# Two modulation steps ahead of the first projection, keys split two tiles at a time, the last blocks' product with v and the last norm by halves

## The chip, the core and the metric

The kernel runs on one core of a Trainium2 chip. A core has four engines that compute: TensorE (PE: matmuls and transposes, with weight loads listed apart as PEld), VectorE (DVE), ScalarE (ACT) and GpSimd (POOL). SyncE (SP) issues most transfers. Each engine takes its instructions in the order of its own list and waits on semaphores that other engines or transfers raise. The time is device microseconds for one launch of the program; before is the median of 3 runs.

## What is computed

One layer of a hybrid backbone block over 512 latent and 256 context tokens of width 1024, all in f32. Cut to what matters here:

```python
mod = silu(c) @ w_mod + b_mod            # shift, scale, gate; twice
h = x * (1 + sc1) + sh1                  # and the context with its own
z = h @ w_in                             # q, k, v, o, gates of the mLSTM; q, k, v of the attention
hm = mlstm_bidir(silu(conv(z_qk)), z_v, gates)
qa, ka = rope(rms_norm(z_qa)), rope(rms_norm(z_ka))
att = softmax(qa @ ka.T * scale) @ va    # 8 query heads, 2 heads of keys
mix = concat([sigmoid(o) * norm(hm), att]) @ w_out
x = layer_norm(ALPHA * x + g1 * mix)
y = peer(x * (1 + sc2) + sh2)            # per token: gelu(u[idx] . x) * g, times v[idx]
x = layer_norm(ALPHA * x + g2 * y)
```

PEER looks up, for each token, 8 x 16 of 16384 experts; each expert has a row u (dotted with the token) and a row v (added, weighted).

## The kernel before

Tokens lie in tiles of 128 (`NCH` = 6 with the context, `NT` = 4 latent). The kernel is one long program written in stages; within a stage a scheduler has already interleaved the engines' instructions, so the lists below are what each engine runs.

**Projections.** `ORDER` (L71) is a string of steps, each run in turn. K, A, B, Q, R, C, D, O and P are column groups of `w_in` (K: keys and values of the attention and the gates; A to D: the mLSTM's q and k, with the convolution on DVE; Q and R: the attention's q; O and P: the output gate, with a sigmoid on ACT). `load_cols` loads 1 MB into a slot `wi` (L206), ACT casts it to a high part `whi` (L208), POOL subtracts to get a low part `wlo` (L209), each in two halves, and PE makes three products (high x high, high x low, low x high; L219). The step m is `mod_rows`: a 1 MB load `wm` of the modulation's weights (L419) into the same three `wi` slots, and two products with a running sum on DVE, `mod_col` (L151). There are 16 such steps; those not in `ORDER` follow at its end (`more_rows(16)`). g and s are the gates' and the states' parts of the mLSTM; k and q are norm and rope of the attention's keys and queries, on DVE, with Newton steps for the reciprocal root (L96 to L103). g ends with `amax` (L354) on DVE, which PE turns in `pc` (L357). Ahead of K, PE computes `pv`, the values of the mLSTM, which ACT copies to `vaug` (L293).

**Attention and mLSTM output.** `keys(c)` (L504 to L516) prepares one tile of keys: ACT casts (L509) and DVE subtracts (L510) into `kd`, a tile of two buffers, each high and low part written twice side by side; PE transposes four times into `pkk` (L513), and ACT copies to `khh` and `kll` (L515, L516). Then come `queries` (`qd` on ACT and POOL, `pq` on PE) and the logits `pS` (L537). Mixed in is the mLSTM's `inner`: `pst` (L597), `stt` (L600), four `dm` operations on DVE (L606), an exponential on ACT (L608) and a product on POOL (L609).

**PEER's sum.** `blocks` goes through 29 blocks of experts for each of four token tiles. A block is gathered into `uv` (rows u and v side by side), its weights `wt` are made on PE, ACT and DVE, and `add` multiplies by v into `py`, a tile of two halves of 512 columns in PSUM (L1211). After the last block of the last tile `finish` (L1247) multiplies by g2, adds ALPHA times x (L1253, L1254), takes the statistics in two halves (`moments`, L738) and normalises (L1258, L1259).

## Time and profile before

| | us |
|---|---|
| median of 3 runs (1197.64 to 1202.17) | 1198.37 |
| the profiled execution | 1204.68 |
| its span in the trace | 1202.9 |
| projections and mLSTM states | about 71 to 226 |
| keys, and the first logits | about 226 to 246 |
| attention | about 246 to 340 |
| last `py` matmul to the end of the span | 1189.0 to 1202.9 |

A row of the timeline gives the start, the length, the engine, the line, the operation with output <- inputs and the shape, and in brackets how long the engine stood idle before it and what it waited for. `x4` after a row means that so many like it run together and share the length.

### The profile page before, as it was taken

What the parts mean: (1) busy time and instruction counts of PE and PEld (TensorE: products, weight loads), DVE (VectorE), ACT (ScalarE), POOL (GpSimd) and SP (SyncE); (2) the same over time, 40 slices, a digit from 0 to 9 for tenths busy, and PEclk for the clock granted to TensorE, in tenths of its full rate; (3) what the DMA queues carried; (4) which work ended last, traced back from release to release, by engine and by line L of the source; (5) the groups of instructions that cost most, each with busy time, mean ns of one, the idle gap of its engine ahead of it and who ended that gap; (6) DMA issues with size and microseconds to landing.
All of it is one profiled execution on the core that took longest, in us unless ns stands there. A gap on an engine that the chain in (4) does not pass through costs nothing.

```text
span 1202.9 us, 19211 instructions
## 1 busy us (share of the span) xinstructions
PE 1038.4 (86%) x6784; PEld 837.7 (70%) x6784; DVE 826.4 (69%) x2698; ACT 464.8 (39%) x1132; POOL 465.7 (39%) x374
## 2 busy tenths in 40 slices
...
GB/s 364 226 202 217 168 177 36 74 80 15 1 102 173 159 274 252 172 39 108 384 249 305 280 299 371 330 333 286 339 401 282 301 280 285 417 318 340 377 315 115
DMA packets 109038, 284.15 MB, mean 236 GB/s; under 512 B 9316, under 2 KB 62280, under 8 KB 92936
## 3 DMA queue, kind: packets, MB, share of 16 engines
...
q8 instruction: 55, 0.90, 0.3%
q14 instruction: 47, 0.39, 0.1%
HBM read 237.17 MB, written 45.66 MB: 235 GB/s over the span
## 4 chain that ended last, share of the span: by engine, by line
PE 38%; DVE 16%; DMA 10%; issue 8%; ACT 2%; SPq 1%; POOL 1%; another core or an unknown queue 0%; DVEq 0%; ACTq 0%; POOLq 0%
PE py L1211 8%; PE pwq L839 8%; PE s L1301 4%; DMA xg<-h2d,ti 4%; PE pW L1031 3%; PE pw L770 2%; PE put L1287 2%; PE po L542 2%; DMA Wd<-work 2%; DVE work L900 2%; DMA uv<-in_uv,ri 2%; DVE work L899 1%; DVE work L902 1%; DVE work L901 1%; PE pf L1028 1%
## 5 line engine op out<-in xcount | busy, mean ns | idle before, releaser
L1211 PE MATMUL py<-uv,wt 128*128 128x512 f32 x464 | 239.7, 636 | 14.6 <-DVE wt L1303 7.8
L1122 POOL DMA_INDIRECT uv<-in_uv,ri x116 | 119.1, 1026 | 133.4 <-PE py L1211 65.0
L1301 PEld LDWEIGHTS s<-ht,ut 128*128 128x128 f32 x1088 | 141.4, 202 | 37.1 <-ACT wt L1302 18.3
L1301 PE MATMUL s<-ht,ut 128*128 128x128 f32 x1088 | 151.5, 289 | 14.8 <-ACT wt L1302 13.9
L1122 POOL DMA_INDIRECT wr<-Wd,wi x116 | 125.6, 1083 | 69.5 <-issue 35.6
L1211 PEld LDWEIGHTS py<-uv,wt 128*128 128x128 f32 x464 | 83.1, 203 | 70.0 <-issue 53.8
L1288 ACT COPY ut<-put 128x512 f32<-128x512 f32 x136 | 75.2, 588 | 102.3 <-PE put L1287 72.1
L1031 PEld LDWEIGHTS <-A 128*128 128x128 f16 x1024 | 89.7, 146 | 20.3 <-issue 13.1
L1033 ACT ACTIVATE work<-pW 128x512 f32<-128x512 f32 x128 | 73.5, 597 | 78.2 <-PE pW L1031 66.5
L1031 PE MATMUL pW<-B,A 128*128 128x128 f16 x1024 | 95.3, 225 | 6.4 <-ACT work L1033 2.9
L1287 PEld LDWEIGHTS put<-cst,uv 128*128 128x128 f32 x544 | 68.3, 152 | 41.8 <-issue 29.9
L1122 POOL DMA_INDIRECT xg<-h2d,ti x48 | 57.9, 1206 | 94.1 <-DVE ti L1163 44.6
L839 PE MATMUL pwq<-h2T,wq 128*128 128x256 f32 x416 | 94.2, 379 | 0.0
L1287 PE MATMUL put<-cst,uv 128*128 128x128 f32 x544 | 80.3, 291 | 15.4 <-DMA uv<-in_uv,ri 13.0
L1183 DVE SCALAR_TENSOR_TENSOR xg<-xg,uv 128x1024 f32<-128x1024 f32 x48 | 58.5, 1219 | 46.5 <-DMA xg<-h2d,ti 46.4
L839 PEld LDWEIGHTS pwq<-h2T,wq 128*128 128x128 f32 x416 | 77.0, 190 | 9.4
L1021 DVE TENSOR_TENSOR B<-B,igr 128x1024 f16<-128x1024 f16 x128 | 82.9, 687 | 1.0
L1018 DVE TENSOR_TENSOR A<-iob,ig 128x1024 f16<-128x1024 f16 x64 | 44.0, 688 | 47.6 <-ACT ig L1004 27.8
L1028 PE MATMUL pf<-B,A 128*128 128x128 f16 x512 | 75.0, 226 | 1.1 <-issue 1.0
L209 POOL TENSOR_TENSOR wlo<-wi,whi 128x1024 fp32r<-128x1024 f32 (+1 forms) x18 | 47.9, 2675 | 60.6 <-ACT whi L208 60.5
L1028 PEld LDWEIGHTS <-A 128*128 128x128 f16 x512 | 60.5, 147 | 8.4 <-issue 6.4
L1303 DVE TENSOR_TENSOR wt<-wt,wr 128x128 f32<-128x128 f32 x68 | 19.6, 289 | 58.1 <-ACT wt L1302 58.1
...
## 6 DMA issues: line engine op xcount, KB each, us to landing
...
```

The lines of the kernel that those rows point to most:

```text
L209: nc.gpsimd.tensor_tensor(lo[:, k:k + 4, 0:cw], wv[:, k:k + 4], hi[:, k:k + 4, 0:cw].bitcast(F32), op=ALU.subtract)
L839: nc.tensor.matmul(pt, w[:, k, :], h2T[:, k, t0 * P:(t0 + 2) * P], start=k == 0, stop=k == KC - 1)
L1021: nc.vector.tensor_tensor(B[:, q].rearrange("p a n r -> p a (n r)"), (B[:, 0] if q else ior).rearrange("p a n r -> p a (n r)"), igr[:, q, ...
L1028: nc.tensor.matmul(pf[:, 0:P], A[:, :, n], B[:, 0, :, n, :], start=c == 0 and n == 0, stop=c == P // TCH - 1 and n == TCH - 1)
L1031: nc.tensor.matmul(pw[:, (n - n4) * P:(n - n4 + 1) * P], A[:, :, n], B[:, q, :, n, :], start=q == 1, stop=q == 2)
L1033: nc.scalar.mul(Wn[:, :, n0 + n4:n0 + n4 + 4], pw.rearrange("p (n k) -> p k n", n=4), 1.0 / GSC)
L1122: nc.gpsimd.indirect_dma_start(out=dst, out_offset=None, in_=src, in_offset=bass.IndirectOffsetOnAxis(ap=ids, axis=0))
L1183: nc.vector.scalar_tensor_tensor(xg, xg, 1.0, w[:, 0:D], op0=ALU.mult, op1=ALU.mult, accum_out=nf)
L1211: nc.tensor.matmul(py[:, hs], wt, w[:, D + half * 512:D + half * 512 + 512], start=i == 0, stop=i == n - 1)
L1287: nc.tensor.transpose(pt[:, q * P:(q + 1) * P], w[:, (4 * kh + q) * P:(4 * kh + q + 1) * P], ident)
L1288: nc.scalar.copy(ut[:, 4 * kh:4 * kh + 4, :], pt.rearrange("p (q n) -> p q n", q=4))
L1301: nc.tensor.matmul(s_[:, 0:P], ut[:, k, :], ht[:, k, :], start=k == 0, stop=k == KC - 1)
```

## The change

It has four parts. `ORDER` puts two steps m ahead of K and rearranges those behind it (14 in the string instead of 15, so that two follow at the end instead of one). `keys` takes two tiles of tokens at a time, so that one cast or subtraction covers both; the buffer is twice as wide. For the last token tile `add` holds back the products of the last three blocks and then issues all three for the first half of `py` and all three for the second. `finish` does its multiplication, addition and statistics half by half.

```diff
--- before.py
+++ after.py
@@ -51,6 +51,7 @@
 
 UVB = 7
 LATE = 5
+TAIL = 3
 XGB = 3
 LOOK = 5
 LB = 3
@@ -68,7 +69,7 @@
 DMB = 3
 STEPS = (1, 2)
 MRB = 2
-ORDER = "KmgAmmgBmmgmkgQmmRmsmmmsCqmDmOmP"
+ORDER = "mmKmgAmgBgkmgQmmRmsmmmsCqmDmOmP"
 ON_DVE = (1, 3, 5, 6, 7)
 WARM = 20
 W1 = 272
@@ -501,19 +502,21 @@
     khh = ap_.tile([P, 2, TOK], F32R, name="khh")
     kll = ap_.tile([P, 2, TOK], F32R, name="kll")
 
-    def keys(c):
-        k3 = ka[:, c].rearrange("p (h n) -> p h n", h=2)
-        kd = ap_.tile([P, 2, 2, 2, 64], F32, tag="qd", name=f"kd{c}", bufs=2)
+    def keys(c0):
+
+        k3 = ka[:, c0:c0 + 2].rearrange("p c (h n) -> p c h n", h=2)
+        kd = ap_.tile([P, 2, 2, 2, 2, 64], F32, tag="qd", name=f"kd{c0}", bufs=2)
         kd_r = kd.bitcast(F32R)
         for r in range(2):
-            nc.scalar.copy(kd_r[:, 0, :, r], k3)
-            nc.vector.tensor_tensor(kd_r[:, 1, :, r], k3, kd[:, 0, :, r], op=ALU.subtract)
-        pt = bank(f"pkk{c}", "t")
-        for i in range(4):
-            nc.tensor.transpose(pt[:, i * P:(i + 1) * P], kd[:, i // 2, i % 2].rearrange("p r n -> p (r n)"), ident)
-        cs = slice(c * P, (c + 1) * P)
-        nc.scalar.copy(khh[:, :, cs], pt[:, 0:256].rearrange("p (h n) -> p h n", h=2))
-        nc.scalar.copy(kll[:, :, cs], pt[:, 256:512].rearrange("p (h n) -> p h n", h=2))
+            nc.scalar.copy(kd_r[:, 0, :, :, r], k3)
+            nc.vector.tensor_tensor(kd_r[:, 1, :, :, r], k3, kd[:, 0, :, :, r], op=ALU.subtract)
+        for c in range(2):
+            pt = bank(f"pkk{c0 + c}", "t")
+            for i in range(4):
+                nc.tensor.transpose(pt[:, i * P:(i + 1) * P], kd[:, i // 2, c, i % 2].rearrange("p r n -> p (r n)"), ident)
+            cs = slice((c0 + c) * P, (c0 + c + 1) * P)
+            nc.scalar.copy(khh[:, :, cs], pt[:, 0:256].rearrange("p (h n) -> p h n", h=2))
+            nc.scalar.copy(kll[:, :, cs], pt[:, 256:512].rearrange("p (h n) -> p h n", h=2))
 
     def queries(c):
 
@@ -676,7 +679,7 @@
 
     one, two = scan(), attend()
     next(one)
-    for c in range(NCH):
+    for c in range(0, NCH, 2):
         keys(c)
     swo = ExitStack()
     wop = swo.enter_context(tc.tile_pool(name="wop", bufs=1))
@@ -1205,11 +1208,17 @@
                 py = ps.tile([P, D], F32, tag="y", name=f"py{t}", bufs=1)
                 pys[t] = py
             py = pys[t]
-            w, wt = live[t, i]
+            if t == NT - 1 and n - TAIL <= i < n - 1:
+                return
+
+            js = range(n - TAIL, n) if t == NT - 1 and i == n - 1 else (i,)
             for half in range(2):
                 hs = slice(half * 512, half * 512 + 512)
-                nc.tensor.matmul(py[:, hs], wt, w[:, D + half * 512:D + half * 512 + 512], start=i == 0, stop=i == n - 1)
-            del live[t, i]
+                for j in js:
+                    w, wt = live[t, j]
+                    nc.tensor.matmul(py[:, hs], wt, w[:, D + half * 512:D + half * 512 + 512], start=j == 0, stop=j == n - 1)
+            for j in js:
+                del live[t, j]
             if i == n - 1:
                 if t < NT - 1:
                     y = bp.tile([P, D], F32, tag="fy", name=f"y{t}")
@@ -1250,9 +1259,15 @@
         if loaded:
             xt, lg2, lb2 = loaded
             yt = pool.tile([P, D], F32, tag="fx", name=f"fx{t}")
-            nc.vector.tensor_tensor(yt, y, g2b, op=ALU.mult)
-            nc.vector.scalar_tensor_tensor(xt, xt, ALPHA, yt, op0=ALU.mult, op1=ALU.add)
-            mean, r = moments(pool, xt, f"l2_{t}")
+            bs = pool.tile([P, 2, 6], F32, tag="lbs", name=f"lbsl2_{t}")
+            for h in range(2):
+                hs = slice(h * 512, h * 512 + 512)
+                nc.vector.tensor_tensor(yt[:, hs], y[:, hs], g2b[:, hs], op=ALU.mult)
+                nc.vector.scalar_tensor_tensor(xt[:, hs], xt[:, hs], ALPHA, yt[:, hs], op0=ALU.mult, op1=ALU.add)
+                nc.vector.bn_stats(bs[:, h], xt[:, hs])
+            mvt = pool.tile([P, 2], F32, tag="lmv", name=f"lmvl2_{t}")
+            nc.vector.bn_aggr(mvt, bs)
+            mean, r = mvt[:, 0:1], rstd_of(pool, mvt[:, 1:2], LN_EPS, f"l2_{t}")
             for h in range(2):
                 hs = slice(h * 512, h * 512 + 512)
                 nc.vector.scalar_tensor_tensor(yt[:, hs], xt[:, hs], mean, lg2[:, hs], op0=ALU.subtract, op1=ALU.mult)
```

In the new program every line behind the edits stands some lines lower (L151 is L152, L208 is L209, L1211 is L1219). The three places that the prediction speaks of:

**The start of the projections, on ACT.** `whi` is K's high part, `vaug` the copies of the mLSTM's values. Before:

```order
L208 CAST whi_459<-wi_458 128x1088 x2
L293 COPY vaug<-pv_175 128x4x128
L293 COPY vaug<-pv_176 128x4x128
L293 COPY vaug<-pv_177 128x4x128
L293 COPY vaug<-pv_178 128x4x128
L293 COPY vaug<-pv_179 128x4x128
L293 COPY vaug<-pv_180 128x4x128
```

After:

```order
L294 COPY vaug<-pv_175 128x4x128
L294 COPY vaug<-pv_176 128x4x128
L294 COPY vaug<-pv_177 128x4x128
L294 COPY vaug<-pv_178 128x4x128
L294 COPY vaug<-pv_179 128x4x128
L294 COPY vaug<-pv_180 128x4x128
L209 CAST whi_467<-wi_466 128x1088 x2
```

K's two casts have moved behind the six copies. On SP the loads begin m, m, K, m, A, m, B where they began K, m, A, m, m, B; on DVE ten products of m stand ahead of the last copy of the gates (`gat`, L247) instead of eight, 11 instead of 14 between it and `amax`, and 11 instead of 10 behind `amax`.

**The last steps m, on DVE**, in the norm of q. `ssqq` are the sums of squares, `rvq`, `rtq` and `rrq` the Newton steps; `wm_2002` is the last step m in both, `wm_1998` in the new list the one ahead of it. Before:

```order
L434 TENSOR_REDUCE ssqq<-sqq_1616 128x8
L151 SCALAR_TENSOR_TENSOR wm_2002,modT<-wm_2002,crs 128x1024
L96 TENSOR_SCALAR rvq<-ssqq 128x32
L151 SCALAR_TENSOR_TENSOR wm_2002,modT<-wm_2002,crs 128x1024
L98 TENSOR_SCALAR rtq<-rvq 128x32
L474 TENSOR_TENSOR modT<-modT,ccs 128x32
L99 TENSOR_SCALAR rrq<-rtq 128x32
L475 TENSOR_SCALAR modT<-modT 128x8
L101 SCALAR_TENSOR_TENSOR rtq<-rrq 128x32
L102 TENSOR_TENSOR rtq<-rtq,rvq 128x32
```

After:

```order
L152 SCALAR_TENSOR_TENSOR wm_1998,modT<-wm_1998,crs 128x1024
L97 TENSOR_SCALAR rvq<-ssqq 128x32
L102 SCALAR_TENSOR_TENSOR rtq<-rrq 128x32
L103 TENSOR_TENSOR rtq<-rtq,rvq 128x32
L104 SCALAR_TENSOR_TENSOR rrq<-rtq,rrq 128x32
L152 SCALAR_TENSOR_TENSOR wm_2002,modT<-wm_2002,crs 128x1024
L102 SCALAR_TENSOR_TENSOR rtq<-rrq 128x32
L152 SCALAR_TENSOR_TENSOR wm_2002,modT<-wm_2002,crs 128x1024
L103 TENSOR_TENSOR rtq<-rtq,rvq 128x32
L475 TENSOR_TENSOR modT<-modT,ccs 128x32
L104 SCALAR_TENSOR_TENSOR rrq<-rtq,rrq 128x32
L476 TENSOR_SCALAR modT<-modT 128x8
```

The last step's two products have moved from ahead of the Newton steps into them, and the step ahead of it has taken their place.

**The keys, on DVE.** `cv` is the convolution of D; `kd` are the low parts of the keys, of which the new names cover two tiles; `dm` belongs to the mLSTM. Before:

```order
L235 SCALAR_TENSOR_TENSOR cv_512_1765<-pz_True,cwt,cv_512_1765 128x511
L510 TENSOR_TENSOR kd_2047<-ka,kd_2047 128x2x64 x2
L510 TENSOR_TENSOR kd_2059<-ka,kd_2059 128x2x64 x2
L510 TENSOR_TENSOR kd_2071<-ka,kd_2071 128x2x64
L606 SCALAR_TENSOR_TENSOR dm_0_2040<-mr_0_2038,a,cst 128x128 x4
L510 TENSOR_TENSOR kd_2071<-ka,kd_2071 128x2x64
L510 TENSOR_TENSOR kd_2083<-ka,kd_2083 128x2x64 x2
L606 SCALAR_TENSOR_TENSOR dm_1_2124<-mr_1_2122,a,cst 128x128 x4
L510 TENSOR_TENSOR kd_2095<-ka,kd_2095 128x2x64 x2
L606 SCALAR_TENSOR_TENSOR dm_0_2156<-mr_0_2154,a,cst 128x128
L510 TENSOR_TENSOR kd_2107<-ka,kd_2107 128x2x64 x2
```

After:

```order
L236 SCALAR_TENSOR_TENSOR cv_512_1761<-pz_True,cwt,cv_512_1761 128x511
L512 TENSOR_TENSOR kd_2047<-ka,kd_2047 128x4x64 x2
L512 TENSOR_TENSOR kd_2066<-ka,kd_2066 128x4x64 x2
L609 SCALAR_TENSOR_TENSOR dm_0_2040<-mr_0_2038,a,cst 128x128 x4
L512 TENSOR_TENSOR kd_2085<-ka,kd_2085 128x4x64
L609 SCALAR_TENSOR_TENSOR dm_1_2109<-mr_1_2107,a,cst 128x128
L512 TENSOR_TENSOR kd_2085<-ka,kd_2085 128x4x64
L609 SCALAR_TENSOR_TENSOR dm_1_2109<-mr_1_2107,a,cst 128x128 x3
```

The four `dm` operations stood in the middle of the second group of keys (tiles 2 and 3) and now stand between the second and the third.

**The end, on PE and DVE.** On PE, `py` is the sum, `s_28` the dots of block 28; `uv_27` is block 27. Before:

```order
L1287 MATMUL put_28_1_11425<-cst,uv_28_11351 128x128 x4
L1211 MATMUL py_10757<-uv_27_11289,wt_27_11401 128x512 x2
L1301 MATMUL s_28_11436<-ht_10579,ut_28_11418 128x128 x8
L1211 MATMUL py_10757<-uv_11_11318,wt_11_11431 128x512 x2
L1211 MATMUL py_10757<-uv_28_11351,wt_28_11435 128x512 x2
```

After:

```order
L1219 MATMUL py_10742<-uv_27_11274,wt_27_11386 128x512
L1316 MATMUL s_28_11419<-ht_10564,ut_28_11403 128x128 x8
L1219 MATMUL py_10742<-uv_11_11303,wt_11_11416 128x512
L1219 MATMUL py_10742<-uv_28_11336,wt_28_11418 128x512
L1219 MATMUL py_10742<-uv_27_11274,wt_27_11386 128x512
L1219 MATMUL py_10742<-uv_11_11303,wt_11_11416 128x512
L1219 MATMUL py_10742<-uv_28_11336,wt_28_11418 128x512
```

One half of block 27 now comes ahead of block 28's dots and the other behind them, with the halves of blocks 11 and 28. On DVE, with what each row waits for in brackets (a semaphore of PE, of DVE itself, or of a transfer); `fx` is the product with g2, `xl` the sum, `lbsl` the statistics. Before:

```order
L1253 TENSOR_TENSOR fx_11451<-py_10757,g2b 128x1024 [waits DMAHW7_49,PE_49]
L1254 SCALAR_TENSOR_TENSOR xl<-xl,fx_11451 128x1024 [waits DMAHW0_49,DVE_49]
L738 BN_STATS lbsl_3_11454<-xl 128x6 [waits DVE_49]
L738 BN_STATS lbsl_3_11454<-xl 128x6
L740 BN_AGGR lmvl_3_11457<-lbsl_3_11454 128x2 [waits DVE_49]
```

After:

```order
L1265 TENSOR_TENSOR fx_11436<-py_10742,g2b 128x512 [waits DMAHW7_49,PE_49]
L1265 TENSOR_TENSOR fx_11436<-py_10742,g2b 128x512
L1266 SCALAR_TENSOR_TENSOR xl<-xl,fx_11436 128x512 [waits DMAHW0_49,DVE_49]
L1266 SCALAR_TENSOR_TENSOR xl<-xl,fx_11436 128x512 [waits DVE_49]
L1267 BN_STATS lbsl_3_11437<-xl 128x6 [waits DVE_49] x2
L1269 BN_AGGR lmvl_3_11444<-lbsl_3_11437 128x2 [waits DVE_49]
```

Of the two half multiplications the first waits for PE and the second for nothing more.

## The prediction

> **What bounds the kernel now.** I read the page first (engine shares and the chain that ended last), then the list of waits for the places where PE stands still longest, then busy time by window for the stages that the edits touch, then the timeline there.
>
> ```profile
> span 1202.9 us, 19211 instructions
> PE 1038.4 (86%) x6784; PEld 837.7 (70%) x6784; DVE 826.4 (69%) x2698; ACT 464.8 (39%) x1132; POOL 465.7 (39%) x374
> PE 38%; DVE 16%; DMA 10%; issue 8%; ACT 2%; SPq 1%; POOL 1%; another core or an unknown queue 0%; DVEq 0%; ACTq 0%; POOLq 0%
> ```
>
> PE is the busiest engine, but the edits lie where it waits. The windows (columns: length, busy time of PE, PEld, DVE, ACT, POOL with counts, granted clock, DMA share, GB/s) show which engine sets each stage.
>
> ```profile
> 108.00:125.00 17.00, 17.00 (x100) 14.89 (x100) 15.10 (x24) 3.13 (x5) 5.83 (x2) 1.00 0.58 193
> 131.30:140.86 9.56, 0.00 (x1) 0.03 (x1) 9.12 (x25) 4.66 (x18) 5.50 (x7) 0.75 0.66 230
> 180.00:226.00 46.00, 46.00 (x300) 41.81 (x298) 44.13 (x112) 12.41 (x17) 14.74 (x8) 1.00 0.07 24
> 235.00:240.00 5.00, 2.26 (x9) 1.52 (x10) 5.00 (x16) 3.14 (x10) 2.02 (x3) 0.50 0.22 75
> 240.00:246.00 6.00, 4.20 (x18) 3.48 (x17) 1.84 (x4) 4.40 (x11) 4.89 (x4) 0.50 0.87 256
> 252.00:300.00 48.00, 46.27 (x379) 43.79 (x377) 40.93 (x143) 28.71 (x62) 8.12 (x7) 1.00 0.09 29
> ```
>
> Through the projections PE and DVE are both full, and DVE ends last: PE stands still for 9.56 us until `amax`. From 235 to 246 us, while the attention's keys are prepared, PE works 6.46 of 11 us. From 252 us on it is full again, so what the keys gain or lose is passed on.
>
> **Part 1, the order.** Two modulation steps go ahead of projection K. No load is added; each step is one 1 MB load and two products on DVE.
>
> ```profile
> 68.99 5.00 POOL L209 TENSOR_TENSOR wlo<-wi,whi 128x1088 fp32r<-128x1088 f32 x2
> 70.15 3.04 ACT L293 COPY vaug<-pv 128x512 f32<-128x512 f32 x6 [1.32 <-PE pv L289]
> 74.04 0.39 PE L219 MATMUL pn<-wlo,hhi 128*128 128x272 f32 x1 [0.70 <-POOL wlo L209]
> 75.61 0.18 DVE L247 COPY gat<-pn 128x16 f32<-128x16 f32 x1 [3.95 <-PE pn L219]
> 78.96 1.79 DVE L151 SCALAR_TENSOR_TENSOR wm<-wm,crs 128x1024 f32<-128x1024 f32 x1 [3.17 <-DMA wm<-in_w_modT]
> 120.40 1.23 DVE L151 SCALAR_TENSOR_TENSOR wm<-wm,crs 128x1024 f32<-128x1024 f32 x1 [1.90 <-DMA wm<-in_w_modT]
> 164.65 1.89 DVE L151 SCALAR_TENSOR_TENSOR wm<-wm,crs 128x1024 f32<-128x1024 f32 x1 [1.43 <-DMA wm<-in_w_modT]
> 140.86 0.66 PE L357 MATMUL pc<-cst,amax 64*128 64x64 f32 x2 [9.56 <-DVE amax L354]
> ```
>
> K's casts on ACT, until now ahead of the six `vaug` copies, stand behind them in the new order. Those copies end at 73.19, so POOL can begin K's low part near 74.3 where it began at 68.99: about 5 us later, and with it PE's K and the projections behind it. That is hidden as long as DVE sets `amax`: of PE's 9.56 us of standing still, some 4.5 remain. The cover gone, it costs up to 5.
>
> DVE: ahead of the last `gat` copy stand 10 products instead of 8, where DVE idles (3.95 and 3.17 us above). From there to `amax` they are 11 instead of 14: 3 x 1.22 = 3.66 us less. K's 5 us come on top: 5 - 3.66 = +1.3, or -0.6 if the 1.90 us wait also goes. I take **+0.4**; the ends are -0.6 and +5.
>
> Behind `amax` 11 products stand instead of 10: **+1.2** (2.4 if the one saved earlier fell into a wait). The last pair is now inside the Newton steps of q's norm.
>
> ```profile
> 188.52 0.37 SPq L419 DMA_DIRECT2D wm<-in_w_modT  x1
> 196.05 2.43 POOL L209 TENSOR_TENSOR wlo<-wi,whi 128x1024 fp32r<-128x1024 f32 x1
> 202.52 0.19 DVE L101 SCALAR_TENSOR_TENSOR rtq<-rrq 128x32 f32<-128x32 f32 x1
> 227.13 0.49 PE L597 MATMUL pst<-qkT 128*128 128x128 f32 x2 [0.92 <-ACT qkT L237]
> 228.39 0.94 ACT L467 ACTIVATE om<-pn 128x256 f32<-128x256 f32 x3
> ```
>
> Its load needs the slot that this POOL operation frees at 198.5 (before, it was issued at 188.52). A 1 MB load alone takes an estimated 4.9 us (1024 KB at the windows' best rates of 200 to 250 GB/s), so it lands near 203.4; DVE gets there near 202.1, ahead of the last step's 202.52: a wait of **+1.3**, bounds 0 and 4.9. All of q's rope and D's convolution queue behind it on DVE, and the keys behind those. One sigmoid of P leaves the stretch ahead of the keys: -0.3 (three took 0.94). PE's own wait for D's convolution, 0.92 until 227.13, grows by 2.9 to some 3.8. Sum of part 1: 0.4 + 1.2 + 1.3 - 0.3 = **+2.6**; its ends are 0.3 and 12.
>
> **Part 2, the keys.** Six casts and six subtractions of 128x256 replace twelve and twelve of 128x128; transposes and copies stay.
>
> ```profile
> 229.20 0.90 ACT L509 CAST kd<-ka 128x128 fp32r<-128x128 f32 x4
> 229.76 1.21 PE L513 MATMUL pkk<-cst,kd 128*128 128x128 f32 x8 [2.14 <-ACT kd L509]
> 230.51 5.04 POOL L649 TENSOR_TENSOR om<-om,mw 128x512 f32<-128x512 f32 x4 [20.96 <-DMA mw<-in_mhw]
> 230.57 0.37 ACT L515 CAST khh<-pkk 128x256 fp32r<-128x256 f32 x1
> 230.83 0.38 ACT L516 CAST kll<-pkk 128x256 fp32r<-128x256 f32 x1
> 233.09 3.14 DVE L606 SCALAR_TENSOR_TENSOR dm<-mr,a,cst 128x128 f32<-128x128 f32 x4
> 236.49 1.11 PE L513 MATMUL pkk<-cst,kd 128*128 128x128 f32 x4 [3.45 <-DVE kd L510]
> 238.85 2.06 PE L513 MATMUL pkk<-cst,kd 128*128 128x128 f32 x8 [1.25 <-ACT kd L509]
> 242.66 0.80 PE L620 MATMUL pnum<-vaug,dm 128*128 128x129 f32 x2 [1.75 <-ACT stt L600]
> 245.56 0.99 PE L537 MATMUL pS<-khh,qst 128*128 128x512 f32 x2
> ```
>
> The gain is not the fewer instructions but the queue: now two of the three groups are subtracted ahead of DVE's four `dm` operations, which run 3.14 us beside POOL's `om`; before, the second group was cut by them. DVE should begin `dm` near 231.2 and end near 234.3; the third group then waits for one more `dm` (about 0.8) and is ready near 235.3, its eight transposes (2.06 as before) done at 237.4 instead of 240.9. That is -3.5; the wider casts give back an estimated 0.3 (a cast of 128x256 follows another after 0.26, 230.83 - 230.57; four of 128x128 took 0.90). I take **-3.2**. Bounds: 0, if the chain over POOL's `qd` sets the first logits anyway, and -6.5, PE's waits of 3.45, 1.25 and 1.75 all gone.
>
> The clock stood at 0.50 from 235 to 246 us, behind PE's 3.45 us wait; a shorter wait there may keep it up (second rival), the 3.8 us ahead of the keys may bring it down sooner. By the Trainium skill, "TensorE: Matmul & The Clock Gate", section "Part 1: The HAM clock gate (the "warmup" mystery)", an idle window of about 3.4 us halves the clock; the trace agrees with 3.45 us and 0.50. By that rule the sum would be rival 2's if the wait in the keys goes below that window, and the forecast's if the wait ahead of the keys goes above it.
>
> **Part 3, the tail.**
>
> ```profile
> 1181.86 1.88 PE L1211 MATMUL py<-uv,wt 128*128 128x512 f32 x4
> 1184.67 0.40 ACT L1200 ACTIVATE wt<-wr,nf 128x128 f32<-128x128 f32 x1
> 1185.36 3.60 PE L1211 MATMUL py<-uv,wt 128*128 128x512 f32 x8
> 1189.00 1.23 DVE L1253 TENSOR_TENSOR fx<-py,g2b 128x1024 f32<-128x1024 f32 x1 [2.84 <-PE py L1211]
> 1190.26 1.22 DVE L1254 SCALAR_TENSOR_TENSOR xl<-xl,fx 128x1024 f32<-128x1024 f32 x1
> 1191.52 1.29 DVE L738 BATCH_NORM_STATS2 lbsl<-xl 128x6 f32<-128x512 f32 x2
> 1196.46 1.41 DVE L1259 SCALAR_TENSOR_TENSOR fx<-fx,rrl,lnr 128x512 f32<-128x512 f32 x2
> ```
>
> Halves would pay if DVE worked on half 0 while PE adds half 1. The new order does not let it: only the first multiply waits for PE and the second has no wait of its own, so that one wait covers all of `py`. What remains is cost. PE used to add block 27 whole ahead of block 28's dots; now one half of it lies behind them: five half products (two records each) after the gate at 1185.07, where four took 3.60. One is (3.60 - 1.88) / 2 = 0.86, the start perhaps 0.2 earlier: +0.65. On DVE four 512-wide operations at 1.41 a pair stand for two 1024-wide ones at 1.26 from start to start: 2.82 - 2.52 = +0.3. Together **+0.9**; ends +0.3 and, if the halves do overlap, -1.1 (the multiply, the add and the statistics of half 0 gone from the end, 2.0, against the 0.9).
>
> **Sum.** 2.6 - 3.2 + 0.9 = +0.3. The profiled execution took 1204.68 us (1.78 outside its span), 6.3 above the median of 1198.37; I carry the difference over unchanged: **1198.7 us**, no change that can be told. About 0.5% (6 us) is what a measurement of this kernel can tell from none, and the runs of before themselves span 4.5 us.
>
> **Rivals.**
> 1. *The late K passes through* (slower). Place: DVE's `amax`. If the products moved into DVE's idle time only return as waits for loads, `amax` moves by the whole 5 us, 4.6 more than forecast: 1203.3; and the last pair's load, late as well, may cost its full 4.9 where I took 1.3: **1206.9**. It decides once `amax` comes later than 145 us in the new trace. For it: DVE already waits 6.5 us in three places for such loads (3.17, 1.90 and 1.43 above), and the slots are three. Against: DVE sheds 3.66 us of work there. Chance 0.22.
> 2. *The clock stays up in the keys* (faster). The eight last transposes at 1.21 instead of 2.06 (0.85), and half of the 4.20 us that PE works at 0.50 from 240 to 246 (2.1): 2.9 less, **1195.8**; with the last pair's wait and K's +0.4 gone too, 1194.1. For it: the third group waits about 2 us. Against: the 3.8 us ahead of the keys. Chance 0.20.
> 3. *The halves overlap*, as the edit's text says: 1198.7 - 2.0 = **1196.7**. The order speaks against it. Chance 0.08.
>
> **How the numbers follow.** The forecast keeps 0.50. Slower by over 0.5% (above 1204.4) is half of rival 1 and 0.03 of the forecast's upper side: 0.14. Faster (below 1192.4) needs rival 2 together with most of the bound of -6.5 on the keys: 0.06, and 0.06 for the same without the clock: 0.12. Within: 0.74. The range 1192 to 1205.5 takes in rivals 2 and 3 and most of rival 1; corners of several bounds at once stay out.
>
> **What would show it.** Part 1: K's first matmuls near 74 to 77 us, the wait before `pc` down to about 5 us, `amax` within 1.5 us of 140.5, and a DMA wait ahead of a product of L152 near 202. Part 2: no wait of 3.4 us for `kd`, one block of `dm` behind four subtractions, the first logits 3 us nearer to D's last convolution. Part 3: the first half multiply starting after the last `py` matmul, PE's end and DVE's end later by 0.6 and 0.9 relative to block 27's product. I am wrong if the first logits come over 3 us away from 245, or if the stretch from 340 to 1178 us, which no edit touches, changes length.

## The result, and the profile after

The change makes the kernel slower: 1211.18 us is the median of 11 runs (1208.17 to 1215.85), against 1198.46 for 11 runs of the kernel before beside them. The ratio is 1.0107 (95% interval 1.0084 to 1.0131), some 12.7 us. The forecast was 1198.7, with 1192 to 1205.5 as its range.

The profiled execution took 1208.17 us, 3.0 below its median, while that of before (1204.68) lay 6.2 above its own. The two traces therefore differ by only 3.5 us at their ends, and the loss has to be read along the way: a milestone of the one against the same milestone of the other. The differences are those of the rounded times.

| start of, in us | before | after | difference |
|---|---|---|---|
| last `pv` matmul | 70.9 | 70.7 | -0.2 |
| first matmul of projection K | 71.1 | 74.1 | +3.0 |
| last copy of the gates (`gat`) | 91.0 | 97.4 | +6.4 |
| `amax` | 140.4 | 145.8 | +5.4 |
| last `vw` (states of the mLSTM) | 178.6 | 185.6 | +7.0 |
| first cast of the keys | 229.2 | 239.2 | +10.0 |
| last transpose of the keys | 240.5 | 247.6 | +7.1 |
| first logits `pS` | 245.6 | 254.2 | +8.6 |
| first matmul of the output projection (`pw`) | 365.5 | 376.3 | +10.8 |
| first `py` | 612.0 | 622.8 | +10.8 |

All of this loss is there before PEER's sum begins. The page of after (span 1206.4 us) shows none of it in its busy times: PE works 1035.5 us instead of 1038.4, DVE 829.8 instead of 826.4.

**Up to `amax`.** First the list of what DVE waited for from 64 to 150 us, of before (time, times, longest):

```profile
DVE gat L247 <- PE pn L219: 7.7, 4, 4.0
DVE wm L151 <- DMA wm<-in_w_modT: 5.1, 2, 3.2
```

and of after:

```profile
DVE gat L248 <- PE pn L220: 11.5, 3, 8.2
DVE wm L152 <- DMA wm<-in_w_modT: 8.7, 4, 3.4
```

The forecast let two products fill DVE's idle time ahead of `gat`. They do run there, but DVE then waits longer for the late K (11.5 us instead of 7.7) and longer for loads (8.7 instead of 5.1). PE still stands still for 9.3 us ahead of `pc`, where some 5 were forecast. The timeline of after shows both:

```profile
74.07 0.39 PE L220 MATMUL pn<-whi,hhi 128*128 128x272 f32 x1 [2.94 <-ACT whi L209]
74.10 4.95 POOL L210 TENSOR_TENSOR wlo<-wi,whi 128x1088 fp32r<-128x1088 f32 x2 [4.49 <-ACT whi L209]
76.64 0.59 PE L220 MATMUL pn<-wlo,hhi 128*128 128x272 f32 x1 [1.81 <-POOL wlo L210]
77.04 0.43 PE L220 MATMUL pn<-whi,hhi 128*128 128x272 f32 x1
82.03 0.18 DVE L248 COPY gat<-pn 128x16 f32<-128x16 f32 x1 [8.16 <-PE pn L220]
117.71 2.10 DVE L152 SCALAR_TENSOR_TENSOR wm<-wm,crs 128x1024 f32<-128x1024 f32 x1 [3.07 <-DMA wm<-in_w_modT]
```

K's low part begins at 74.10 instead of 68.99, 5 us late as forecast, and K's first matmul is 3.0 us late. But PE has now waited twice, 2.94 and 1.81 us, and it goes on at half the clock. Windows of before and of after (columns as in the prediction: length; PE, PEld, DVE, ACT, POOL; clock, DMA share, GB/s):

```profile
77.00:82.00 5.00, 5.00 (x42) 5.00 (x41) 3.04 (x6) 0.63 (x3) 2.39 (x1) 1.00 0.96 362
```

```profile
77.00:82.00 5.00, 5.00 (x23) 5.00 (x23) 0.00 (x0) 0.00 (x0) 2.05 (x1) 0.50 0.31 95
```

PE does 23 matmuls in these five us instead of 42. The clock stands at 0.50 from 75.6 to 82.4 us, which costs about 3.4, and the last copy of the gates ends 6.4 us later than before (97.62 instead of 91.21). From there to the end of `amax`, before:

```profile
91.21:140.72 49.51, 40.09 (x250) 35.77 (x248) 45.12 (x82) 18.10 (x38) 18.60 (x11) 0.95 0.68 234
L151 DVE SCALAR_TENSOR_TENSOR wm<-wm,crs 128x1024 f32<-128x1024 f32 x14 | 21.5, 1544 | 1.9 <-DMA wm<-in_w_modT 1.9
```

After:

```profile
97.62:146.06 48.44, 39.27 (x243) 34.95 (x241) 40.98 (x75) 17.69 (x37) 17.66 (x11) 0.94 0.57 196
L152 DVE SCALAR_TENSOR_TENSOR wm<-wm,crs 128x1024 f32<-128x1024 f32 x11 | 15.7, 1432 | 5.3 <-DMA wm<-in_w_modT 5.3
```

The second line is the group of the products: busy time, mean ns, and the idle time ahead of them. DVE has 4.1 us less to do, as the three products fewer promised (3.66). But it is idle for 7.5 us instead of 4.4, because the loads' waits grow from 1.9 to 5.3. So only 1.1 of the 6.4 us comes back, and the 5.3 that are left are the 5.4 of the table but for rounding.

**Behind `amax`.** From the end of `amax` to the first cast of the keys, before, with the products' group:

```profile
140.66:229.20 88.54, 79.93 (x543) 74.42 (x543) 81.19 (x258) 32.48 (x62) 26.93 (x14) 0.95 0.22 75
L151 DVE SCALAR_TENSOR_TENSOR wm<-wm,crs 128x1024 f32<-128x1024 f32 x10 | 14.2, 1439 | 1.4 <-DMA wm<-in_w_modT 1.4
```

After:

```profile
146.06:239.20 93.14, 81.94 (x550) 75.74 (x550) 81.64 (x259) 33.17 (x62) 25.79 (x14) 0.92 0.23 82
L152 DVE SCALAR_TENSOR_TENSOR wm<-wm,crs 128x1024 f32<-128x1024 f32 x11 | 17.1, 1567 | 4.4 <-DMA wm<-in_w_modT 4.4
```

The stage is 4.6 us longer: 1.6 of it up to the last `vw` (39.5 us instead of 37.9) and 3.0 from there to the keys (53.6 instead of 50.6). The loads' waits grow by 3.0 us. The products take 2.9 us more, of which one product is 1.2; but DVE as a whole is busy only 0.45 us longer, because other operations of this stage are shorter than before (the product of `qa` with `qw` takes 2.7 us instead of 7.1). The stage's loss is idle time of DVE, not longer work.

**What stretches a product.** The long products lie beside POOL's subtractions, most of them beside `wlo` (timeline of after; `x2` is two halves):

```profile
83.70 5.75 POOL L210 TENSOR_TENSOR wlo<-wi,whi 128x1024 fp32r<-128x1024 f32 x2 [4.65 <-ACT whi L209]
85.15 2.04 DVE L152 SCALAR_TENSOR_TENSOR wm<-wm,crs 128x1024 f32<-128x1024 f32 x1
87.12 3.40 DVE L152 SCALAR_TENSOR_TENSOR wm<-wm,crs 128x1024 f32<-128x1024 f32 x1
137.14 4.70 POOL L210 TENSOR_TENSOR wlo<-wi,whi 128x1024 fp32r<-128x1024 f32 x2 [0.29 <-ACT whi L209]
137.56 2.07 DVE L346 TENSOR_TENSOR cm<-cm 32x127 f32<-32x127 f32 x1
```

The product of 87.12 ends at 90.52, which is 1.07 after POOL's row (83.70 + 5.75 = 89.45): it looks as if it had stood until POOL was done and then run. The first step of `cm`, 32x127, takes 2.07 us where the third, 32x126, takes 0.37. The prediction's own rows of before already had it (1.79 and 1.89 us beside the usual 1.22), and it was passed over. Before also had three products of 2.70 to 2.76 us up to `amax`, against five of 2.04 to 3.40 after; which operation meets a subtraction shifts with the order.

This is what the Trainium skill states in "SBUF — State Buffer", section "SBUF: two separate sides": a VectorE operation with two inputs in SBUF and a GpSimd operation that reads SBUF take turns on one pair of ports, for a whole instruction each. The trace agrees with it (2.0 to 3.5 us instead of 1.22).

**The keys.** Timeline of after:

```profile
247.22 0.66 PE L516 MATMUL pkk<-cst,kd 128*128 128x128 f32 x4 [1.62 <-DVE kd L512]
249.00 0.63 ACT L611 ACTIVATE dm<-dm 128x512 f32<-128x512 f32 x1
249.54 1.12 ACT L526 CAST qd<-qa 128x512 fp32r<-128x512 f32 x2
252.45 1.97 PE L532 MATMUL pq<-cst,qd 128*128 128x128 f32 x8 [4.57 <-POOL qd L527]
254.24 1.01 PE L540 MATMUL pS<-khh,qst 128*128 128x512 f32 x2
```

The wait of 3.45 us for `kd` is gone; 1.62 is left. From the first cast to the end of the transposes it is 8.6 us instead of 11.7, the 3 us of the forecast. But a wait has taken its place: q's cast on ACT stands behind the exponential of `dm`, and PE waits 4.57 us for `qd`. From the end of the transposes to the logits it is 6.4 us instead of 4.7. The first logits come at 254.2, so the prediction's own sign of an error, logits over 3 us away from 245, was there.

**The tail.** Timeline of after:

```profile
1186.12 1.95 PE L1316 MATMUL s<-ht,ut 128*128 128x128 f32 x16
1187.90 4.56 PE L1219 MATMUL py<-uv,wt 128*128 128x512 f32 x10
1192.50 1.29 DVE L1265 TENSOR_TENSOR fx<-py,g2b 128x512 f32<-128x512 f32 x2 [3.79 <-PE py L1219]
1200.63 0.34 SPq L1275 DMA_DIRECT2D out<-fx  x1
```

The first half multiplication starts behind the last `py` matmul: nothing overlaps. From block 28's dots to the first store of the output it is 1200.63 - 1186.12 = 14.51 us; before, 1197.24 - 1183.58 = 13.66. The 0.85 is all PE's: from the dots to the end of the last `py` it is 6.34 us instead of 5.38, and from the first multiplication to the store 8.13 instead of 8.24.

### The profile page after: what moved, and what is told of

Same layout as the page of the kernel before. It is cut to its first block, busy times and chain, and to the rows that moved or that the text cites. A ratio compares the mean times of both kernels' runs of the same rounds, so it can differ in the third digit from the quotient of the medians.

```text
span 1206.4 us, 19199 instructions
## 1 busy us (share of the span) xinstructions
PE 1035.5 (86%) x6784; PEld 835.9 (69%) x6784; DVE 829.8 (69%) x2694; ACT 464.7 (39%) x1126; POOL 469.0 (39%) x374
## 4 chain that ended last, share of the span: by engine, by line
PE 31%; issue 13%; DMA 13%; DVE 12%; ACT 3%; POOL 2%; SPq 1%; another core or an unknown queue 1%; POOLq 0%; DVEq 0%; ACTq 0%
PE pwq L842 7%; PE py L1219 6%; DMA Wd<-work 5%; PE s L1316 3%; DMA wr<-Wd,wi 3%; PE pw L773 2%; PE pW L1034 2%; PE po L545 2%; DMA xg<-h2d,ti 2%; PE ppt L571 1%; DVE work L905 1%; DVE work L903 1%; PE put L1302 1%; DVE work L902 1%; SPq L1041 1%
## 5 line engine op out<-in xcount | busy, mean ns | idle before, releaser
L1219 PE MATMUL py<-uv,wt 128*128 128x512 f32 x464 | 235.6, 627 | 12.5 <-DVE wt L1318 4.6
L1125 POOL DMA_INDIRECT uv<-in_uv,ri x116 | 124.9, 1077 | 134.0 <-PE py L1219 65.2
L1316 PE MATMUL s<-ht,ut 128*128 128x128 f32 x1088 | 152.3, 291 | 18.2 <-ACT wt L1317 13.8
L1125 POOL DMA_INDIRECT wr<-Wd,wi x116 | 122.8, 1059 | 67.3 <-issue 38.3
L1219 PEld LDWEIGHTS py<-uv,wt 128*128 128x128 f32 x464 | 81.4, 199 | 66.4 <-issue 56.3
L1302 PEld LDWEIGHTS put<-cst,uv 128*128 128x128 f32 x544 | 65.1, 147 | 38.3 <-issue 22.3
L1125 POOL DMA_INDIRECT xg<-h2d,ti x48 | 57.6, 1199 | 85.5 <-DVE ti L1166 37.4
L1302 PE MATMUL put<-cst,uv 128*128 128x128 f32 x544 | 76.6, 282 | 13.9 <-DMA uv<-in_uv,ri 10.5
L152 DVE SCALAR_TENSOR_TENSOR wm<-wm,crs 128x1024 f32<-128x1024 f32 x32 | 49.2, 1558 | 13.1 <-DMA wm<-in_w_modT 13.1
```

Of the source, the lines that this page charges most:

```text
L152: nc.vector.scalar_tensor_tensor(jk, w, 1.0, crs[:, j, :], op0=ALU.mult, op1=ALU.mult, accum_out=modT[:, m, j:j + 1])
L1125: nc.gpsimd.indirect_dma_start(out=dst, out_offset=None, in_=src, in_offset=bass.IndirectOffsetOnAxis(ap=ids, axis=0))
L1219: nc.tensor.matmul(py[:, hs], wt, w[:, D + half * 512:D + half * 512 + 512], start=j == 0, stop=j == n - 1)
L1302: nc.tensor.transpose(pt[:, q * P:(q + 1) * P], w[:, (4 * kh + q) * P:(4 * kh + q + 1) * P], ident)
L1316: nc.tensor.matmul(s_[:, 0:P], ut[:, k, :], ht[:, k, :], start=k == 0, stop=k == KC - 1)
```

## The experiments

Each ratio compares with runs of the kernel before on the same chip; those took 1180.91 us for e1 to e4 and for e9 to e12, 1201.37 for e5 to e8, 1180.69 for e15 to e17, and 1191.82 in a single run for e13 and e14. All versions compute the same output.

| | us | ratio to before | 95% interval |
|---|---|---|---|
| e1 order alone | 1193.97 | 1.0107 | 1.0081 to 1.0133 |
| e2 keys alone | 1184.52 | 1.0029 | 1.0009 to 1.0049 |
| e3 tail alone | 1182.89 | 1.0009 | 0.9989 to 1.0028 |
| e4 all but the order | 1185.33 | 1.0026 | 1.0006 to 1.0047 |
| e5 new order, K loaded and cast first | 1209.40 | 1.0068 | 1.0042 to 1.0094 |
| e6 new order, one m more ahead of B | 1212.75 | 1.0096 | 1.0068 to 1.0124 |
| e7 old order, one m ahead of K | 1208.10 | 1.0061 | 1.0036 to 1.0087 |
| e8 tail with `py` in two tiles | 1195.07 | 0.9951 | 0.9925 to 0.9978 |
| e9 the same as e8, again | 1172.73 | 0.9934 | 0.9910 to 0.9958 |
| e10 the same, one block held back | 1176.72 | 0.9954 | 0.9930 to 0.9978 |
| e11 keys alone, q's first step ahead of them | 1181.90 | 1.0013 | 0.9989 to 1.0037 |
| e12 e8 and the keys | 1174.78 | 0.9956 | 0.9928 to 0.9983 |
| e13 new order, all low parts on DVE | 1202.12 | one run | |
| e14 old order, all low parts on DVE | 1195.95 | one run | |
| e15 old order, first five low parts on DVE | 1177.76 | 0.9973 | 0.9949 to 0.9997 |
| e16 e8 and e15 | 1171.28 | 0.9930 | 0.9902 to 0.9957 |
| e17 new order, first five low parts on DVE | 1187.79 | 1.0059 | 1.0032 to 1.0086 |

### Which part makes the loss

e1 takes the string alone, e2 the diff of `keys` and its loop alone, e3 that of `add` and `finish` alone, and e4 the changed kernel with the old string:

```diff
# e1, on the kernel before
-ORDER = "KmgAmmgBmmgmkgQmmRmsmmmsCqmDmOmP"
+ORDER = "mmKmgAmgBgkmgQmmRmsmmmsCqmDmOmP"
# e4, on the changed kernel
-ORDER = "mmKmgAmgBgkmgQmmRmsmmmsCqmDmOmP"
+ORDER = "KmgAmmgBmmgmkgQmmRmsmmmsCqmDmOmP"
```

> Before with the new string ORDER alone; keys, add and finish as before. Theory 1 (the order of the projections is the whole loss: K starts late and DVE does not catch up): 9 to 13 us slower than before (about 1208 to 1211), amax near 146, the first cast of kd about 10 us later than before's 229.2. Theory 2 (the order costs the 2.6 us of my prediction in a typical run, the rest comes from the keys and the attention behind them): 2 to 4 us slower. Theory 3 (the middle of the kernel, which no edit touches, runs slower when it starts later): 5 to 7 us slower here, and the time from the first py matmul to the last is longer than before's 576.

> Before with the keys taken two tiles at a time, alone. Theory 1: the eight last transposes end 3 us earlier after the first cast of kd (8.6 instead of 11.7 us), but the first logits only 1 to 1.5 us earlier, and the attention gives that back: within 2 us of before. My prediction's term: 3.2 us faster. Theory 2: 3 to 6 us slower, because the attention's instructions stand in another order.

> Before with the last three blocks' product with v and the last norm by halves, alone. All theories: 0.9 us slower (0.65 on PE, 0.3 on DVE); the first half multiplication starts after the last py matmul. If the halves overlapped: 1.1 us faster.

> The changed kernel with the old string ORDER: keys and tail as changed. Theory 1: within 2 us of before (about 1198 to 1200). Theory 2: 4 to 7 us slower. My prediction's terms added: 2.3 us faster.

The string alone gives a loss with the same ratio as the change. (e1 and e4 together would be 1.33%; the change has 1.07, with 1.31 as its upper bound.) In e1 `amax` comes at 145.0 (140.0 in e3, on the same chip), the keys' first cast at 240.3 (228.8) and `pw` at 375.6 (364.8): +5.0, +11.5 and +10.8.

The keys are no gain but 0.29% slower. That is 3.6 us between the medians, more than the first theory of e2 allowed and within the range of its second, an attention in another order. e4, with keys and tail, loses 4.4 us, which is the second theory's range too. The keys do their part: their last transposes end some 3 us earlier. But the attention gives it back. Its exponential of logits, timeline of e2, first and twelfth:

```profile
247.18 0.90 ACT L560 ACTIVATE pe<-pS,mx 128x768 f32<-128x768 f32 x1 [0.20 <-DVE mx L558]
...
289.55 0.90 ACT L560 ACTIVATE pe<-pS,mx 128x768 f32<-128x768 f32 x1 [0.22 <-DVE mx L558]
```

and of e3, where the keys are the old ones:

```profile
249.13 0.90 ACT L559 ACTIVATE pe<-pS,mx 128x768 f32<-128x768 f32 x1 [2.58 <-DVE mx L557]
...
287.93 0.90 ACT L559 ACTIVATE pe<-pS,mx 128x768 f32<-128x768 f32 x1 [0.22 <-DVE mx L557]
```

The first is 1.95 us earlier in e2, the twelfth 1.62 later. Part of these 3.6 us is the clock, which is 0.50 from 283.6 to 287.0 us in e2 and 1.00 in e3. In e4, which has the same keys, the clock stays up there: from the first to the twelfth it takes 41.0 us, where e2 takes 42.4 and e3 38.8. So about 1.4 us are the clock's and 2.2 the attention's. No run shows which of its instructions costs them. The tail's cost of 0.09% (about 1 us) lies inside its interval and agrees with the 0.9 forecast.

### How the order loses up to `amax`: the late K, or the late loads

e5 keeps the new string but loads and casts K ahead of it; e6 gives A its second m back, so that the last m stand where they stood; e7 puts one m ahead of K and leaves the rest.

```diff
# e5: new string, and
+    first = load_cols(1536, 272)
     for ch in ORDER:
-        "K": lambda: proj_N(1536, 272, range(NCH), ev_kv),
+        "K": lambda: proj_N(1536, 272, range(NCH), ev_kv, first),
# e6
+ORDER = "mmKmgAmmgBgmkgQmmRmsmmmsCqmDmOmP"
# e7
+ORDER = "mKmgAmmgBmmgmkgQmmRmsmmmsCqmDmOmP"
```

> e1_order with K's load and casts issued ahead of the two steps m, so that K's casts stand on ACT ahead of the six vaug copies again; all else as in e1_order (13 us slower than before, amax at 145.0, first cast of kd at 240.3). Theory K (K's late casts push everything): amax back at 140 to 141.5, PE's first product of K near 71, first cast of kd 232 to 234, 3 to 5 us slower than before. Theory S (the three slots: the loads of the modulation come late whatever K does): amax stays at 144 to 146 and the kernel 9 to 13 us slower.

> e1_order with the step m that the new string lacks put back behind A (mmKmgAmmgBgmkgQ...), so that one step is left for the end as before, not two; K's casts stay behind the vaug copies. If the last pair inside q's Newton steps costs 3 to 4 us: amax as in e1_order (145 to 147), from amax to the first cast of kd 89 to 92 us instead of 95.3, 8 to 10 us slower than before. If the pair costs nothing: 95 us and 13 us slower.

> Before with one step m put ahead of K and nothing else moved (16 in the string, none left for the end). K's casts stand behind the vaug copies, as in e1_order. Theory K: amax 143 to 146; since no pair is left for q's Newton steps, the first cast of kd 2 to 3 us less far from amax than before's 88.8: 1 to 4 us slower. Theory S: amax 140 to 142 (one slot less disturbed), and 1 to 3 us faster.

Against e3 `amax` comes 2.3 us later in e5, 7.7 in e6 and 4.6 in e7. Counted from the last `pv` it is 2.6 in e5 and 3.8 in e7.

e5 shows late loads without a late K. K is on time there (first matmul 70.3, last copy of the gates at 90.2, in e3 at 90.5). Behind that copy, e3 and then e5:

```profile
90.74:140.32 49.58, 40.10 (x250) 35.78 (x248) 45.15 (x82) 18.10 (x38) 18.63 (x11) 0.95 0.66 233
L152 DVE SCALAR_TENSOR_TENSOR wm<-wm,crs 128x1024 f32<-128x1024 f32 x14 | 21.5, 1543 | 1.9 <-DMA wm<-in_w_modT 1.9
```

```profile
90.45:142.58 52.13, 39.37 (x244) 35.05 (x242) 44.24 (x79) 17.30 (x37) 18.65 (x11) 0.92 0.60 215
L151 DVE SCALAR_TENSOR_TENSOR wm<-wm,crs 128x1024 f32<-128x1024 f32 x13 | 19.7, 1522 | 5.1 <-DMA wm<-in_w_modT 5.1
```

DVE is idle for 7.9 us instead of 4.4 and busy for 0.9 less. DVE waits for loads as long as in the change (5.1 us, there 5.3), and that alone costs more than the one product fewer saves.

e7 shows a late K without late loads. DVE's waits up to 150 us:

```profile
DVE gat L247 <- PE pn L219: 14.6, 6, 8.1
DVE wm L151 <- DMA wm<-in_w_modT: 2.7, 3, 1.5
```

DVE waits for loads less than in e3 (2.7 us instead of 5.4), but K's casts stand behind the `vaug` copies again (first matmul 74.5). Here too the clock is halved at once, from 75.1 to 81.9 us. The last copy of the gates comes 5.5 us later, counted from the last `pv`; behind it stand 13 products instead of 14, and 3.8 us arrive at `amax`. So K's lateness passes through but for the work that is taken from behind it, and the waits for loads come on top. All three slots are taken by m, m and K: A's load goes out at 70.52 in the change, at 57.80 before.

The halved clock belongs to the late K: it is there between 73 and 83 us in all six traces in which K's casts stand behind the `vaug` copies (the change, e1, e6, e7, e13, e17), for 3.4 or 6.8 us, and in none of the others. By the medians e6 and e7 lost more than was expected and e5 fell between its two theories: 8.0 us in e5 (3 to 5 if K was the cause, 9 to 13 if the slots were), 11.4 in e6 (8 to 10) and 6.7 in e7 (1 to 4).

e6 and e7 also show the last pair's share: in both it stands ahead of the Newton steps again, and from the last `vw` to the first cast of the keys it is 50.6 us (e6) and 48.8 (e7); e3 has 50.6, e1, e5 and the change 53.6. It cost 3.0 us, where 2.5 were forecast (1.3 of wait and one product of 1.2). The rest of the loss behind `amax`, up to the last `vw`, is 1.6 us in the change and 3.5 in e1.

### The second half of the loss, and POOL's subtractions

e13 and e14 subtract all low parts of `w_in` on DVE, under the new order and the old; e15 to e17 only those of the first five loads.

```diff
# e13, e14
-            nc.gpsimd.tensor_tensor(lo[:, k:k + 4, 0:cw], wv[:, k:k + 4], hi[:, k:k + 4, 0:cw].bitcast(F32),
+            nc.vector.tensor_tensor(lo[:, k:k + 4, 0:cw], wv[:, k:k + 4], hi[:, k:k + 4, 0:cw].bitcast(F32),
# e15, e16, e17
-            nc.gpsimd.tensor_tensor(lo[:, k:k + 4, 0:cw], wv[:, k:k + 4], hi[:, k:k + 4, 0:cw].bitcast(F32),
+            eng = nc.vector if i < 5 else nc.gpsimd
+            eng.tensor_tensor(lo[:, k:k + 4, 0:cw], wv[:, k:k + 4], hi[:, k:k + 4, 0:cw].bitcast(F32),
```

> The new ORDER string alone, and the low parts wlo of w_in subtracted on DVE instead of POOL, so that POOL reads no big tile while the modulation's products run. Two theories of why VectorE was busy 2.1 us longer up to amax with one product fewer (58.6 against 56.6 us). Port: a product or a cm step that meets a POOL subtraction has to wait for it; then all products up to amax take 1.21 to 1.25 us here (in the changed kernel five took 2.04 to 3.40). Rival, traffic: loads or ACT stretch them; then at least three still take over 1.7 us. DVE gets about 10 more operations of an estimated 1.3 us (1.22 for 1024 elements, scaled to 1088), so amax itself may come up to 6 us later or earlier by 1; the sum says little, the durations decide.

> The kernel before with the low parts wlo subtracted on DVE instead of POOL; the partner of e13. Port theory: no product over 1.25 us (before: 1.79, 2.70, 2.76 and 2.75), and the new order's cost at amax, e13 minus e14, is 2 to 4 us, less than the 5.0 to 5.4 measured with POOL, since the stretched operations' share goes while the late K and the waits for loads stay. Traffic theory: the long products stay and the cost stays at 5.0 to 5.4.

> The kernel before with the low parts of the first five loads of w_in (K, A, B, Q, R) subtracted on DVE and the later ones on POOL again. With all low parts on DVE, amax came at 130.4 us where the kernel before has it at 140.4, and the first cast of the keys at 225.1 where it has 229.2. Port theory: amax near 130 again, every product up to amax at 1.21 to 1.45 us; the gain at the keys' first cast lies between 4 us (as with all on DVE) and 10 us (all of amax); the time 4 to 10 us less than before, ratio 0.992 to 0.997. Rival: the earlier amax is given back on PE, which has the same matmuls to do, or in the later stages: ratio 0.998 to 1.002.

> The two PSUM tiles for py (ratio 0.9934 to 0.9956 so far) with the low parts of the first five loads on DVE. The two edits lie in stages 400 us apart: if both gains are passed on, 0.985 to 0.991; if the early one is given back, as that of the keys was, 0.993 to 0.996.

> e15 with the new ORDER string. In single runs with all low parts on DVE the new order cost 4.7 us at amax and 3.8 us at the keys' first cast and at the projection of the output (with POOL: 5.0, 10 and 10.8). If part of the order's loss behind amax comes from VectorE meeting POOL's subtractions, e17 against e15 is 3 to 6 us slower, less than the 12.7 us of the change with POOL; if it doesn't, 10 us or more.

The durations speak for POOL, and against the loads and ACT, which were left as they were. Groups of e14 from 64 to 150 us:

```profile
L151 DVE SCALAR_TENSOR_TENSOR wm<-wm,crs 128x1024 f32<-128x1024 f32 x24 | 28.7, 1223 | 0.8 <-DMA wm<-in_w_modT 0.8
L209 DVE TENSOR_TENSOR wlo<-wi,whi 128x1024 fp32r<-128x1024 f32 (+1 forms) x10 | 12.8, 1304 | 3.6 <-ACT whi L208 3.6
```

No product takes over 1.22 us up to `amax` but one of 1.41, which starts beside POOL's small `sqk`; in e13 likewise, with one more of 2.87 at 67.51, beside POOL's `hlo`, which was not moved. And with 10.5 us of work more on DVE up to there (eight of the ten subtractions) `amax` comes at 130.4, ten us earlier than before.

The other expectation of the port theory was wrong: the order's cost at `amax` does not shrink with the stretch. It is 135.1 - 130.4 = 4.7 us without POOL, 5.0 to 5.4 with it. So the stretched products are no part of the order's loss there: K is late in e13 too (5.0 us at the last copy of the gates). From `amax` to the keys' first cast, e13 and then e14:

```profile
135.37:228.90 93.53, 80.55 (x547) 74.48 (x548) 80.64 (x270) 32.76 (x63) 4.13 (x4) 0.93 0.28 91
```

```profile
130.67:225.10 94.43, 79.85 (x541) 73.79 (x542) 82.15 (x272) 32.55 (x61) 4.87 (x6) 0.93 0.26 90
```

Here the new order needs 0.9 us less than the old; with POOL's subtractions it needed 4.6 more (93.14 against 88.54). But the new order is no faster for it, 93.5 us against 93.1; the old one has lost its lead. The stage has two parts. Up to the last `vw` both orders now take 35.8 us, less than before (37.9) and the change (39.5). From there to the keys they take 57.6 and 58.6, where before takes 50.6 and the change 53.6. The last pair's 3.0 us are not seen there, in a part that has become 4 to 8 us longer for both. So e13 and e14 do not show that POOL's subtractions are the second half. For its first part they may be, but e13 has no wait for a load in the stage either, so the runs do not tell the two apart.

e17 was to tell whether the first five loads are enough, and they are not: against e15 it costs 1187.79 - 1177.76 = 10.0 us, the "10 or more" of its expectation. In the traces the order costs 4.8 us at `amax`, 5.7 at the last `vw` and 8.5 at the keys' first cast. The 2.7 us that are added last are the last pair's again (53.4 us in that part, 50.7 in e15). Stretched products do not explain the difference, since both kernels have three of them behind `amax` (1.97 to 3.38 us in e15, 2.82 to 3.47 in e17).

So of the 4.6 us, 3.0 are the last pair's, as e6 and e7 show, and the 1.6 up to the last `vw` stay open. e15 itself gains 0.27%, less than its port theory had it (0.3 to 0.8%): of the ten us at `amax` about 3 are left at the keys, since from `amax` to the last `vw` it takes 44.6 us where before takes 37.9.

### Halves that do overlap

e8 is e3 with `py` as two tiles of 512 columns in place of one of 1024; copies and the fallback path go by halves too. e9 is the same kernel on another chip, and e10 differs in one number.

```diff
-                py = ps.tile([P, D], F32, tag="y", name=f"py{t}", bufs=1)
-                pys[t] = py
+                pys[t] = [ps.tile([P, 512], F32, tag=f"y{q}", name=f"py{q}_{t}", bufs=1) for q in range(2)]
...
-                    nc.tensor.matmul(py[:, hs], wt, w[:, D + half * 512:D + half * 512 + 512], start=j == 0, stop=j == n - 1)
+                    nc.tensor.matmul(py[half], wt, w[:, D + half * 512:D + half * 512 + 512], start=j == 0, stop=j == n - 1)
...
-            nc.vector.tensor_tensor(yt[:, hs], y[:, hs], g2b[:, hs], op=ALU.mult)
+            nc.vector.tensor_tensor(yt[:, hs], y[h], g2b[:, hs], op=ALU.mult)
# e10, besides
-TAIL = 3
+TAIL = 1
```

> e3_tail with py as two PSUM tiles of 512 columns instead of one of 1024 (and the copy of py for the first three token tiles in two halves). My account (the one tile made half 0 wait for half 1's last matmul): the first half multiplication starts about 1.7 us ahead of the last py matmul's end, DVE's end relative to block 28's dots 1.5 to 2.0 us earlier than in e3_tail, 1 us faster than before. If the wait was not the tile's: as e3_tail, 1 to 2 us slower.

> The kernel of e8_two_tiles once more. Its trace shows the end 1.4 us shorter than the changed kernel's and 0.5 us shorter than before's, yet the comparison gave 5.9 us less than before. If that was the chance of its runs: 0.5 to 2 us faster than before. If two PSUM tiles gain elsewhere: 4 to 8 us faster again.

> e8_two_tiles with TAIL = 1: two PSUM tiles and the last norm by halves, but each block's two half products side by side, as before. The end: half 1 is done one half product (0.86 us) behind half 0 instead of three, and block 27 is added whole ahead of block 28's dots: DVE's end relative to block 28's dots 0 to 0.6 us later than in e8. Time within 1 us of e9_two_tiles_again.

Timeline of e8:

```profile
1183.97 4.56 PE L1215 MATMUL py<-uv,wt 128*128 128x512 f32 x10
1185.99 0.69 DVE L1262 TENSOR_TENSOR fx<-py,g2b 128x512 f32<-128x512 f32 x1 [1.42 <-PE py L1215]
1188.57 0.69 DVE L1262 TENSOR_TENSOR fx<-py,g2b 128x512 f32<-128x512 f32 x1 [0.43 <-PE py L1215]
```

Now each half has a wait of its own, and the first is multiplied 2.5 us before PE ends. From the dots to the store it is 13.15 us, 1.36 less than in the change and 0.5 less than before. That is little beside the gain of the whole kernel, 0.49% in e8 and 0.66% in e9 (6.3 and 8.2 us between the medians).

The rest seems to lie in PEER's sum ahead of the last block. Chips differ, so the traces are compared on one chip each, from the first `py` to the last: 556.4 us in e11 (one tile) against 550.6, 552.6 and 550.3 in e9, e10 and e12 (two tiles), and 556.8 in e15 against 552.2 in e16. That is 3.7 to 6.1 us less with two tiles. e8's own trace does not show it: it has 579.7 us, where e5 to e7 on the same chip have 574.9 to 580.1; but it was the slowest of e8's 12 runs, 8 us above their median. Two tiles let the next token tile's first half begin while the other is still copied, and they also change the order that the scheduler writes there. PE's wait for that copy was small with one tile (0.2 us in sum in e3), so most of the gain must have another source. Which one is open.

e10 shows that holding back blocks brings nothing: with one block the end, from the dots to DVE's last operation, takes 13.6 us as in e9 (13.8 in e8), where up to 0.6 more was expected. Its median is 4 us above e9's, against an expected 1, but the two intervals overlap.

### The keys again

e11 is e2 with q's preparation ahead of the keys, so that its cast does not queue behind `dm`; e12 is e8 with the keys' diff.

```diff
     next(one)
-    for c in range(NCH):
+    next(two)
+    for c in range(0, NCH, 2):
         keys(c)
...
-        for _ in range(STEPS[i % len(STEPS)]):
+        for _ in range(STEPS[i % len(STEPS)] - (i == 0)):
```

> e2_keys with the first tile of queries split ahead of the keys instead of behind them. If POOL's qd behind the keys is what keeps the first logits back (e2 waits 4.5 us for it): the first logits 2 to 3 us earlier after the first instruction of the stage than in e2, and 1 to 3 us faster than before. If the attention is bound by PE's total work from there on: first logits earlier, but the end of the attention within 1 us of e2's, 1 to 4 us slower than before.

> e8_two_tiles with the keys two at a time: the changed kernel with the old ORDER and py in two tiles. By the runs so far keys cost 1 to 3 us: that much slower than e9_two_tiles_again, and within 2 us of before.

In e11 the first logits come at 238.8, 4.4 us earlier than in e2 and 6.4 earlier than in e3. Yet `pw` starts at 364.5, against 365.6 in e2 and 364.8 in e3: of 6.4 us 0.3 arrive. In e12 the keys cost 2.1 us against e9, as expected (1 to 3); but it is 6 us faster than before, not within 2. An earlier start of the attention is worth next to nothing on this kernel.

e16 is the fastest measured, 0.9930, with e9 at 0.9934; their intervals overlap almost wholly, so the gains of e8 and e15 do not add up in a way that these runs can tell. Both beat the kernel before and the changed one.

## Why the prediction was wrong

The forecast was +0.3 us and +12.7 came. At the milestones of the two traces, 5.0 of the difference lie at `amax` (+5.4 against +0.4), 2.4 between `amax` and the keys (+4.6 against 1.2 + 1.3 - 0.3) and 4.0 from the keys to the output projection (+0.8 against -3.2). The last microsecond of the 12.4 is not seen at these milestones.

**Part 1 failed, and with it the sum.** The step that failed is "5 - 3.66": K's 5 us less three products. What came is 6.4 - 1.1.

- *The late K* was to be "hidden as long as DVE sets `amax`". It is not: DVE itself waits for K through `gat` (8.16 us in one row). And 5 us became 6.4, because the clock was halved for 6.8 us at PE's two new waits. e7, where DVE waits less for loads than before, shows K's lateness without them: 5.5 us at the last copy of the gates, 3.8 at `amax`.
- *The three products fewer* were counted as 3.66 us gained. DVE did work 4.1 us less, but 3.1 came back as idle time: the slots are three, and moving two loads ahead makes the next ones late. e5, with K on time, still loses 2.3 us this way.
- *The price of a product*, 1.22 us each, holds only away from POOL's subtractions. This was wrong in the forecast too, but it is not where the loss at `amax` comes from: operations were stretched before as well, and without the stretch (e13, e14) the order costs 4.7 us.

The first two are the first rival, given 0.22: its price for `amax` was 4.6 us above the forecast, and 4.6 to 5.0 came; its point of decision, 145 us, was passed at 145.8. That the price fits so well is partly luck, since the rival knew nothing of the clock. Its upper time, 1206.9, is still too low, because it kept the 3.2 us that the keys were to gain.

The last pair in the Newton steps was right in place and cause, a wait for its load of 1.15 us (forecast 1.3). The second product then met POOL (3.48 us), which was not seen. Timeline of after:

```profile
210.61 1.22 DVE L152 SCALAR_TENSOR_TENSOR wm<-wm,crs 128x1024 f32<-128x1024 f32 x1 [1.15 <-DMA wm<-in_w_modT]
210.79 5.67 POOL L210 TENSOR_TENSOR wlo<-wi,whi 128x1024 fp32r<-128x1024 f32 x2 [5.33 <-ACT whi L209]
214.07 3.48 DVE L152 SCALAR_TENSOR_TENSOR wm<-wm,crs 128x1024 f32<-128x1024 f32 x1
```

PE's wait for D's convolution was 3.05 us in one row and 3.7 in two (forecast 3.8).

**Part 2 was right about the stage and wrong about its worth.** The transposes gained 3.1 us of 3.2 forecast. The step that failed is "what the keys gain or lose is passed on": PE was read as full from 252 us on, and an engine that is full is a reason why an earlier start of part of its work is *not* passed on. e2 ends 0.29% slower and e11 shows 0.3 of 6.4 us arriving. In the change the first logits kept 1.4 of the 3 us (+10.0 at the first cast, +8.6 at the logits), and at `pw` the loss was 10.8 again.

**Part 3 was right**, +0.85 us against +0.9, and so was its reason, one wait for all of the tile: e8 shows it by giving each half its own. Its two terms were off against each other, which is luck: PE took 0.96 us more instead of 0.65 (its own figures, five half products of 0.86 in place of 3.60 and a start 0.2 earlier, come to 0.5), and DVE's halves took 0.1 us less instead of 0.3 more.

**The second and third rivals** did not come as gains. For the second, the last transposes did run at full speed (0.66 us for four, where eight had taken 2.06), and the granted clock was 0.77 and 0.80 while the last keys were made (240 to 246 and 246 to 252 us), where it had been 0.69 and 0.50 (232 to 240 and 240 to 246). But during the new wait of 4.57 us it fell, to 0.72 over 252 to 260, and the logits gained nothing. The forecast also read the 0.50 of before as set by a wait of 3.45 us. In the trace the clock is halved from 235.0, 2.0 us into that wait, and in the change it was halved at 75.6, within K's second wait of 1.81 us. So the length of a single wait did not decide here. The halves did not overlap.

**The other sign that was named** for an error, a stretch from 340 to 1178 us of another length, is no good sign: between the two traces the stretch from the first `py` to the end of the span differs by 7 us (590.9 and 583.6), while in e1 and e3, on one chip, it is 572.8 and 573.0 with different orders ahead.
